# Moving one more group of transposed probabilities from ScalarE and VectorE to GpSimd in the dense attention heads of a two-layer diffusion step

## The chip, the cores and the metric

The kernel runs on one core of a Trainium2 chip. The metric is the time of one execution on the device in microseconds (us); the median of three runs of the kernel before is 3486.17 us.

Engines are named as in the profile: PE is TensorE's matrix products (PEld its weight loads), ACT is ScalarE, DVE is VectorE, POOL (or Pool) is GpSimd, SP issues most DMA transfers. Only ACT and DVE read PSUM in this kernel; Pool works on SBUF alone.

## The reference

Two layers run over 128 prompt tokens and 1024 sample tokens of width 1024. Each layer has an input projection, attention in 16 heads, an output projection and a gated FFN with a width-3 convolution. Six heads are neighbourhood attention (a window of keys for each query); the other ten, called dense here, attend to all keys:

```python
def blocked_attention(q, k, v):
    ...
    def one_block(q_blk):
        s = jnp.einsum('bqhgd,bkhd->bhgqk', q_blk, k).astype(jnp.float32) * scale
        p = jax.nn.softmax(s, axis=-1).astype(v.dtype)
        return jnp.einsum('bhgqk,bkhd->bqhgd', p, v)
```

For a sample token of a dense head there are 1152 keys: 128 cached context keys and 1024 sample keys. Four dense heads are latent attention ("MLA", with head width 96), six are grouped-query attention ("GQA", width 64). All is float32.

## The kernel before, in words

**Precision.** A product of float32 numbers is made of float32r parts: a number is split into a high part (a cast to float32r) and a low part (number minus high part). MLA scores take three products for each block of keys, GQA scores two. The probabilities are split too: both parts of their transpose, `PT[0]` and `PT[1]`, are multiplied with V.

**Phase B (attention, `phase_b`).** Heads follow each other: four MLA, six GQA, six neighbourhood. A dense head works on nine tiles of 128 queries: eight sample tiles in four pairs (tile a = 0 and a = 1 of a pair) and one prompt tile, which comes third. `step` (L915) emits the program for one tile after another in a software pipeline: scores of tile s, exponentials and normalisation of tile s-1, transposes of tile s-3, and pieces of the products with V of older pairs. The tile framework then sets the order of the instructions on each engine, so the order on an engine is not the order in the text of the program.

What a dense tile of 128 queries x 1152 keys needs:

- scores: PE writes 896 columns into a PSUM tile `SA` and 256 into `SB`; DVE takes the maxima (L712 over SA, L789 over SB, the second including the first);
- exponentials: ACT makes exp of SB and of SA into an SBUF tile `P` with sums (L699); Pool adds the two sums (`ssum`, L702); DVE takes the reciprocal (`rs`, L707); Pool multiplies P by it (L708, 1152 columns);
- transposes: PE transposes 128x128 blocks of P into a PSUM bank `T` (L719; two such banks, four blocks in each). The nine blocks of the two tiles of a pair make five groups: a = 0 has blocks 0 to 3 and 4 to 7, a = 1 has the same two, and the fifth group holds block 8 of both tiles (256 columns).
- evacuation of a group: four of the five go through `evac2` (L199): ACT casts T into the high part in PT (L202), DVE subtracts it from T into the low part (L203). The fifth goes `via` SBUF: ACT copies T into `rt` (L724), ACT casts rt into the high part (L194 in `split`), Pool subtracts into the low part (L197);
- products with V: for each block of keys one product for each part of PT, 256 queries wide (L737), into `O`; ACT copies one half of O (`otmp`, L742) and DVE adds the other (Y, L744).

A dense head thus has four via groups and sixteen `evac2` groups of 512 columns, and the prompt tile adds one group of 128 columns. In both layers there are 20 dense heads with 80 pairs.

Outside the dense heads the change touches nothing: neighbourhood heads call `transpose_p` without `via`, and `split` with `hi_eng=pool` has no other caller.

Of the kernel before, what the change touches and what calls it, by code (L numbers as in the profile page):

```python
# [14 lines left out]
F32 = mybir.dt.float32  # L15
# [10 lines left out]
D = 1024  # L26
# [19 lines left out]
def tile_kernel(ctx: ExitStack, tc: tile.TileContext, I, O):  # L46
# [13 lines left out]
    # ---- scratch in DRAM  # L60
    XD = [dram.tile([NTT, 128, D], F32, name=f"XD{i}") for i in range(2 * L - 1)]
    GD = [[dram.tile([2, KC, 128], F32, name=f"GD{l}{i}") for i in range(2)] for l in range(L)]
    # (the two parts of) queries and keys with features on rows, values with tokens on rows;
    # key columns: prompt, cached context, samples
# [7 lines left out]
    # ---- PSUM outside attention: six banks for products, two for transposes and small sums  # L72
# [30 lines left out]
    # ---- helpers  # L103
    nw = ctx.enter_context(tc.tile_pool(name="nw", bufs=3))

    def rsqrt_newton(v, n):
        """v: [128, n], f32; returns its rsqrt, times -8192."""
        u = nw.tile([128, 8], F32, name="nw_u")[:, :n]
        t = nw.tile([128, 8], F32, name="nw_t")[:, :n]
        dve.tensor_scalar(out=u.bitcast(I32), in0=v.bitcast(I32), scalar1=-0.5,  # L110
                          scalar2=float(0x5F3759DF), op0=ALU.mult, op1=ALU.add)
        # y -> y * (3 - y * y * v) / 2 on u = c * y
        c = 1.0
        for _ in range(3):
            if n == 1:
                dve.scalar_tensor_tensor(out=t, in0=u, scalar=u, in1=v, op0=ALU.mult, op1=ALU.mult)  # L116
            else:
                dve.tensor_tensor(out=t, in0=u, in1=u, op=ALU.mult)
                dve.tensor_tensor(out=t, in0=t, in1=v, op=ALU.mult)
            dve.scalar_tensor_tensor(out=u, in0=t, scalar=-3.0 * c * c, in1=u, op0=ALU.add, op1=ALU.mult)  # L120
            c *= -2.0 * c * c
        return u

    def squares(ss, i, src, junk):
        """Sums of squares over the features of a tile of tokens, in two halves, into ss[:, :, i]."""
        for j in range(2):
            act.activation(out=junk[j], in_=src[j], func=AF.Square, accum_out=ss[:, j, i:i + 1])

    def rsqrt_mean(ss, n):
        """From squares: rsqrt of the mean, times -256."""  # L130
        v = nw.tile([128, 8], F32, name="nw_v")[:, :n]
        dve.scalar_tensor_tensor(out=v, in0=ss[:, 0, :n], scalar=D * EPS, in1=ss[:, 1, :n],  # L132
                                 op0=ALU.add, op1=ALU.add)
        return rsqrt_newton(v, n)
# [4 lines left out]
    def h_group(p, tiles, xs, A, B, H, ht_w=256):  # L139
        """h = xs * A + B with features on partitions, in two float32r parts;  # L140
        xs[t]: the scaled tokens [128, D]."""
        hhi, hlo = H
        n, s = 128 * len(tiles), 1 if tiles[0] == 0 else 0
        cs = slice(tiles[0] * 128, tiles[0] * 128 + n)
        for m in range(KC):
            tp = aux()[:, :n]
            for i, t in enumerate(tiles):
                pe.transpose(tp[:, i * 128:(i + 1) * 128], xs[t][:, m * 128:(m + 1) * 128], ident)
            a, b = A[:, m, s:s + 1], B[:, m, s:s + 1]
            act.activation(out=hhi[:, m, cs], in_=tp, func=AF.Identity, scale=a, bias=b)  # L150
            ht = p.tile([128, ht_w], F32, name="ht", bufs=2)[:, :n]
            dve.tensor_scalar(out=ht, in0=tp, scalar1=a, scalar2=b, op0=ALU.mult, op1=ALU.add)
            (pool if m % 2 else dve).tensor_tensor(out=hlo[:, m, cs], in0=ht, in1=hhi[:, m, cs].bitcast(F32),  # L153
                                                   op=ALU.subtract)
            if m % 2:
                yield

    def norm_tiles(p, tiles, src, junk, w, xts, G, xout, A, B, H, xs, groups, eng):
        """x + norm(src) * G for tiles of tokens; lists by tile: src, junk (two halves each),
        w: scratch, then the scaled new x, xts: x; eng: the engines for the gates of each half. When a group of tiles is complete, h."""  # L160
# [38 lines left out]
    def evac2(hi, lo, src, scale=None):  # L199
        """The two parts of src * scale, src in PSUM."""  # L200
        if scale is None:
            act.copy(hi, src)  # L202
            dve.tensor_tensor(out=lo, in0=src, in1=hi.bitcast(F32), op=ALU.subtract)  # L203
        else:
            act.activation(out=hi, in_=src, func=AF.Copy, scale=scale)
            dve.scalar_tensor_tensor(out=lo, in0=src, scalar=scale, in1=hi.bitcast(F32),
                                     op0=ALU.mult, op1=ALU.subtract)

    # ---- adaLN modulation
# [22 lines left out]
    def late_consts(l, z):  # L232
        z.conv = lay.tile([128, 44, 4], F32, name="conv")
        nc.scalar.dma_start(out=z.conv, in_=I["conv"][l])
        z.gtok = lay.tile([128, 896], F32, name="gtok", bufs=1)
        nc.scalar.dma_start(out=z.gtok, in_=I["gtok"][l:l + 1, :].to_broadcast([128, 896]))
        # times -1 / 8192, and the scale of the scores
        for c0, c1, f in ((0, 384, 1.0), (384, 768, 0.125), (768, 896, 1.0)):
            pool.tensor_scalar(out=z.gtok[:, c0:c1], in0=z.gtok[:, c0:c1], scalar1=-f / 8192, scalar2=1.0,
                               op0=ALU.mult, op1=ALU.mult)  # L240

    def ada_done(z, part):
        """The gains and gates, times -1 / 256."""
        gi, dst = {1: (0, z.Am), 2: (1, z.Gm), 4: (2, z.Af), 5: (3, z.Gf)}.get(part, (None, None))
        if dst is not None:
# [5 lines left out]
            else:  # L251
                dve.scalar_tensor_tensor(out=dst, in0=z.mods[:, part], scalar=-1.0 / 256, in1=g,
                                         op0=ALU.mult, op1=ALU.mult)
                # as rows in DRAM
# [7 lines left out]
    def gate_rows(z, p, i):  # L262
        """[128, 2, D]: the gates of samples and prompt on every partition."""
        G = p.tile([128, 2, D], F32, name="G")
        load_gate_rows(z, G, i)
        return G
# [6 lines left out]
    def ada_bias(z, part, c, n, mp):  # L273
        """mods of n chunks of features from mp [128, n, 2] and the biases."""
# [3 lines left out]
    def ada_pe(l, z, p, part, q):  # L278
        """On the tensor engine, four chunks of features: where nothing else can run yet."""
# [14 lines left out]
    def ada_dve(l, z, p, parts, wd):  # L294
        """Sums over the chunks of features on the vector engine, over partitions on TensorE;
        wd columns at a time."""
# [24 lines left out]
    # ---- phase A: input projections  # L321
    def rope_rot(p, x, H, d, tabs, out, eng=dve):
        """x, out: [128, H, d] views; tabs: (cos, signed sin), [128, d] each."""
# [13 lines left out]
    def load_w(wp, src, tag, bufs, lo_eng=pool, wr=None):  # L337
        """The two parts of a block of weights, src [128, a, b]; wr: the pool of the raw ones."""
# [19 lines left out]
    def phase_a(l, z, H, w, before, rest):  # L358
        """w: the weights of the values; before(t): called before token tile t of H is first read;
        rest(): called when w is no longer used, returns the pool for the other weights."""  # L360
# [13 lines left out]
        # values of the grouped-query and the neighbourhood heads  # L374
# [22 lines left out]
        # multi-head latent attention  # L397
# [157 lines left out]
        # neighbourhood attention: q, k, features on partitions  # L555
        with tc.tile_pool(name="an", bufs=1) as p:
            # the cached context
# [57 lines left out]
    # ---- phase B: attention  # L615
    def phase_b(l, Y, kps, bp, pp, sp, bps):
# [5 lines left out]
        def alternating(name, shape):  # L622
            """In one of two pools, in turn."""
# [71 lines left out]
        def exps(P, mneg, pieces, sign):  # L695
            """exp(sign * src + mneg) into P; pieces: (src, first column). Returns the sums."""
# [17 lines left out]
        def transpose_p(blocks, outs, tag="T", via=False):  # L714
            """blocks: columns of P; outs: where they go, one after the other, in the two parts of PT;
            via: through SBUF, for Pool to take a share."""
# [5 lines left out]
            if via:  # L722
                rt = sp.tile([128, 256], F32, name="rt", bufs=2).rearrange("p (a b) -> p a b", b=128)
                act.copy(rt, src)  # L724
                split(rt, *outs)
            else:
                evac2(*outs, src)

        def pv_items(V, PT, slots, n, hg, t0):
            """slots: list of (V tile, PT slot)."""  # L730
# [22 lines left out]
        class Task:  # L753
            """One tile of queries: scores, maximum | exp, 1 / sum | transposes | products with V."""
# [19 lines left out]
            def dense(self, hd, pair, a):  # L774
# [19 lines left out]
                def tr(j):  # L794
                    if a == 0 and j == 0:
                        hd.PT[pair] = new_pt()
                    if j < 8:
                        transpose_p([self.block(j + i) for i in range(4)],
                                    [o[:, j:j + 4, qs] for o in hd.PT[pair]])
# [11 lines left out]
            def na(self, hd, pair, a):  # L811
# [23 lines left out]
                # the blocks of keys by slot of PT; within: the second tile of queries has no slot 4,  # L835
                # the first no slot 6
# [122 lines left out]
    # ---- phase C: output projection  # L959
# [5 lines left out]
    def phase_c(l, z, Y, yst, H, xin, xout, wp):  # L965
        """Returns the generators of the norms that are still to be finished, and their pool's stack."""
# [42 lines left out]
    # ---- phase D: gated ConvFFN  # L1009
    def phase_d(l, z, H, wp, pend, pend_done, last):  # L1010
        """pend: generators that finish the last tiles of H; pend_done(): called when they are,
        returns Y, the pools for convolutions and gated values and the generators to run along;
        last(t, down): called for each tile of Y, down(j) completes a half of it."""
# [15 lines left out]
        def shifted(acc, pts, m, c, sh):  # L1029
            """The products of chunk c, at the column after (sh = 1) or before (sh = -1) their own."""  # L1030
# [91 lines left out]
        # the last gated values chunk by chunk  # L1122
# [75 lines left out]
    def rest_of_norms(owner, gens, done):  # L1198
        """The remaining norms of the layer before, each tile's before it is read."""
# [182 lines left out]
```

## Time and profile before

| what | value |
|---|---|
| median of 3 runs | 3486.17 us (3481.18 to 3488.51) |
| span of the profiled execution | 3484.8 us, 50564 instructions |
| PE busy | 3299.9 us (95%) |
| PEld busy | 2964.7 us (85%) |
| DVE busy | 2220.3 us (64%) |
| ACT busy | 1485.6 us (43%) |
| POOL busy | 1087.5 us (31%) |
| mean granted clock of TensorE | 0.979 of full speed |

The profile is of one execution, whose span from first to last instruction is 3484.8 us, 1.4 us below the median of the runs; no other time of that execution is shown. The shares are over the whole span. The dense heads lie at about 364 to 660 us (layer 1) and 2081 to 2376 us (layer 2), some 17% of it; the rest is projections, neighbourhood heads and the FFN, where the engines stand in quite another proportion.

### The profile page before, as it was taken

The page shows a single profiled execution, that of the slowest core. Times are in us where ns is not written, and L with a number is a line of the kernel's source. Part 1 is how long each engine was busy: PE and PEld are TensorE (multiplying, and loading weights), DVE is VectorE, ACT ScalarE, POOL GpSimd, SP SyncE. Part 2 cuts the span into 40 slices and gives each one's busy share as a digit, 9 for nine tenths or more (in the row PEclk, how much of TensorE's full clock was granted, in tenths as well). Part 3 has the DMA queues.
Part 4 walks back from the last instruction along what each step waited for, and adds up shares of the span by engine and source line. Part 5 has one row for each costly group of instructions (what it writes and reads, how often), then busy time and mean ns, then how long its engine had stood idle before and what let it go on. Part 6 is the DMA issues. An engine that isn't in the chain of part 4 may idle for free. (4 is left out here: it accounts for less than half of the span.)

```text
span 3484.8 us, 50564 instructions
## 1 busy us (share of the span) xinstructions
PE 3299.9 (95%) x18540; PEld 2964.7 (85%) x18540; DVE 2220.3 (64%) x4915; ACT 1485.6 (43%) x3085; POOL 1087.5 (31%) x1063
## 2 busy tenths in 40 slices
PE   7989999999999999999989899999889999999996
PEld 3878888877899999999868789888779999999995
DVE  5785788887755555333588858888776533333437
ACT  4321788884422222222353228888743222222222
POOL 2121445541332223222231314554322222222223
PEclk9999999999999999999999999999999999999998
DMA  6467521453222122111245674215522111111113
GB/s 234 135 186 214 138 72 44 103 145 135 91 67 79 61 67 67 38 43 43 71 159 143 176 231 102 52 44 148 167 91 73 55 49 51 44 44 43 38 37 115
DMA packets 193416, 339.35 MB, mean 97 GB/s; under 512 B 18448, under 2 KB 107920, under 8 KB 193168
## 3 DMA queue, kind: packets, MB, share of 16 engines
q1 hardware_dynamic: 191872, 334.93, 32.6%
q8 instruction: 147, 2.41, 0.3%
q10 hardware_dynamic: 1296, 1.19, 0.1%
q14 instruction: 101, 0.83, 0.1%
HBM read 260.61 MB, written 75.43 MB: 96 GB/s over the span
## 5 line engine op out<-in xcount | busy, mean ns | idle before, releaser
L1025 PE MATMUL mm<-hhi,wu 128*128 128x384 f32 x4224 | 874.5, 336 | 7.3 <-DVE acc L1037 4.5
L1025 PEld LDWEIGHTS mm<-hhi,wu 128*128 128x128 f32 x4224 | 746.4, 188 | 14.5 <-DVE acc L1037 5.0
L1037 DVE SCALAR_TENSOR_TENSOR acc<-mm,conv,acc 128x127 f32<-128x127 f32 (+2 forms) x704 | 314.1, 509 | 359.3 <-ACT acc L1042 359.2
L1072 PE MATMUL aux<-wd,g 128*128 128x512 f32 x2160 | 498.0, 390 | 0.0
L1025 PE MATMUL mm<-hlo,wu 128*128 128x384 f32 x2112 | 496.8, 335 | 0.0
L1072 PEld LDWEIGHTS aux<-wd,g 128*128 128x128 f32 x2160 | 404.7, 188 | 83.1 <-DVE g L1061 0.4
L1025 PEld LDWEIGHTS mm<-hlo,wu 128*128 128x128 f32 x2112 | 379.0, 188 | 0.7 <-DVE hlo L153 0.4
L197 POOL TENSOR_TENSOR wu<-wraw,wu 128x1024 fp32r<-128x1024 f32 x90 | 220.8, 2455 | 442.6 <-ACT wu L194 439.9
L737 PE MATMUL O<-PT,V 128*128 128x256 f32 (+1 forms) x2080 | 345.6, 294 | 6.9 <-DVE Y L744 4.5
L1077 DVE TENSOR_TENSOR Y<-Y,aux 128x512 f32<-128x512 f32 x324 | 220.8, 686 | 200.8 <-PE aux L1072 200.7
L708 POOL TENSOR_SCALAR P<-P,rs 128x1152 f32<-128x1152 f32 (+3 forms) x288 | 290.6, 1010 | 149.8 <-DVE rs L707 123.8
L719 PE MATMUL T<-ident,P 128*128 128x128 f32 x1856 | 299.1, 277 | 17.1 <-DVE PT L203 12.3
L689 PE MATMUL SA<-k,q 128*128 128x512 f32 (+5 forms) x1224 | 301.0, 366 | 8.1 <-ACT ko L611 3.9
L203 DVE TENSOR_TENSOR PT<-T,PT 128x512 fp32r<-128x512 f32 (+1 forms) x448 | 290.3, 656 | 24.9 <-ACT PT L202 18.8
L197 POOL TENSOR_TENSOR wd<-wraw,wd 128x1024 fp32r<-128x1024 f32 x46 | 111.2, 2417 | 612.8 <-ACT wd L194 612.8
L737 PEld LDWEIGHTS O<-PT,V 128*128 128x128 f32 x2080 | 276.7, 189 | 22.3 <-DVE Y L744 10.3
L194 ACT CAST wd<-wraw 128x1024 fp32r<-128x1024 f32 x50 | 52.4, 1050 | 527.9 <-PE aux L1072 400.5
L202 ACT CAST PT<-T 128x512 fp32r<-128x512 f32 (+1 forms) x448 | 247.7, 568 | 55.7 <-PE T L719 42.5
L308 DVE SCALAR_TENSOR_TENSOR aacc<-wadv,sc,aacc 128x512 f32<-128x512 f32 x280 | 234.5, 870 | 46.8 <-DMA wadv<-w_ada 46.7
L719 PEld LDWEIGHTS T<-ident,P 128*128 128x128 f32 x1856 | 213.3, 141 | 58.1 <-DVE PT L203 16.0
L689 PEld LDWEIGHTS SA<-k,q 128*128 128x128 f32 (+1 forms) x1224 | 198.7, 192 | 33.5 <-ACT P L699 6.8
L712 DVE TENSOR_REDUCE mx<-SA 128x1 f32<-128x896 f32 (+1 forms) x192 | 182.3, 950 | 34.5 <-PE SA L689 34.5
(222 smaller groups left out, 5181.9 us busy)
## 6 DMA issues: line engine op xcount, KB each, us to landing
wraw<-w_up SPq DMA_DIRECT2D x88, 512.0 KB, 3.5
wadv<-w_ada SPq DMA_DIRECT2D x160, 256.0 KB, 3.0
wraw<-w_down SPq DMA_DIRECT2D x44, 512.0 KB, 3.5
k<-KT SPq DMA_DIRECT2D x64, 320.0 KB, 5.6
q<-QT SPq DMA_DIRECT2D x48, 288.0 KB, 6.0
XD<-xt SPq DMA_DIRECT2D x27, 512.0 KB, 3.2
xt<-XD SPq DMA_DIRECT2D x27, 512.0 KB, 4.0
wraw<-w_in SPq DMA_DIRECT2D x24, 512.0 KB, 4.0
```

Source lines behind the costliest of these rows:

```text
L197: (lo_eng or pool).tensor_tensor(out=lo, in0=raw, in1=hi.bitcast(F32), op=ALU.subtract)
L202: act.copy(hi, src)
L203: dve.tensor_tensor(out=lo, in0=src, in1=hi.bitcast(F32), op=ALU.subtract)
L308: dve.scalar_tensor_tensor(out=accs[i], in0=w, scalar=sc[:, k, i:i + 1], in1=accs[i], op0=ALU.mult, op1=ALU.add)
L689: pe.matmul(out, q[0:rows, qc:qc + 128], kview(k[0:rows]), start=(i == 0), stop=(i == len(passes) - 1))
L708: pool.tensor_scalar(out=P[:, :n], in0=P[:, :n], scalar1=rs, scalar2=1.0, op0=ALU.mult, op1=ALU.mult)
L719: pe.transpose(tp[:, j * 128:(j + 1) * 128], p, ident)
L737: pe.matmul(op[0][:, :n], V[:, vt, :], PT[e][:, sl, :n], start=(i == 0 and e == 0), stop=(i == last and e == 1))
L1025: pe.matmul(pts[c][:, :CN], a[:, k, :], h_[:, k, c * CN:(c + 1) * CN], start=(k == 0 and a is whi and h_ is hhi), stop=(k == KC - 1 and a ...
L1037: dve.scalar_tensor_tensor(out=d, in0=pts[c][:, lo_ - c * CN:hi_ - c * CN], scalar=cw[:, wi:wi + 1], in1=d, op0=ALU.mult, op1=ALU.add)
L1072: pe.matmul(pt, g[:, ts], d[:, 0, js], start=(n == 0), stop=(n == tot - 1))
L1077: dve.tensor_tensor(out=Y[:, t, js], in0=Y[:, t, js], in1=pt, op=ALU.add)
```

## The change

In the dense heads a second group of each pair goes through SBUF: blocks 4 to 7 of tile a = 0 (512 columns). For via groups, old and new, the high part is now made by Pool (`hi_eng=pool`, a `tensor_copy`, L196) rather than by ACT. `rt` grows from 256 to 512 columns, still with two buffers. Comments and docstrings are removed elsewhere, which moves line numbers by one at most.

```diff
             if via:
-                rt = sp.tile([128, 256], F32, name="rt", bufs=2).rearrange("p (a b) -> p a b", b=128)
+                rt = sp.tile([128, 512], F32, name="rt", bufs=2).rearrange("p (a b) -> p a b", b=128)
+                rt = rt[:, :len(blocks)]
                 act.copy(rt, src)
-                split(rt, *outs)
+                split(rt, *outs, hi_eng=pool)
             else:
                 evac2(*outs, src)
...
                     if j < 8:
                         transpose_p([self.block(j + i) for i in range(4)],
-                                    [o[:, j:j + 4, qs] for o in hd.PT[pair]])
+                                    [o[:, j:j + 4, qs] for o in hd.PT[pair]], via=a == 0 and j == 4)
```

`split` itself is unchanged:

```python
    def split(raw, hi, lo, hi_eng=None, lo_eng=None):
        if hi_eng is None:
            act.copy(hi, raw)
        else:
            hi_eng.tensor_copy(hi, raw)
        (lo_eng or pool).tensor_tensor(out=lo, in0=raw, in1=hi.bitcast(F32), op=ALU.subtract)
```

The order on Pool, in a GQA head of the first layer, from one normalisation to a sum of a later tile. Before (L197 of 256 columns is the fifth group of a pair):

```order
L708 TENSOR_SCALAR P<-P,rs 128x1152
L197 TENSOR_TENSOR PT_5562<-rt,PT_5561 128x256
L702 TENSOR_TENSOR ssum<-ssum 128x1
L708 TENSOR_SCALAR P<-P,rs 128x1152
L702 TENSOR_TENSOR ssum<-ssum 128x1
L708 TENSOR_SCALAR P<-P,rs 128x1152
L197 TENSOR_TENSOR PT_5659<-rt,PT_5658 128x256
```

and with the change, for the same pair (its PT tiles are numbered 5597 and 5598 here) and the next:

```order
L196 CAST PT_5597<-rt 128x4x128
L197 TENSOR_TENSOR PT_5598<-rt,PT_5597 128x4x128
L702 TENSOR_TENSOR ssum<-ssum 128x1
L708 TENSOR_SCALAR P<-P,rs 128x1152
L196 CAST PT_5597<-rt 128x256
L197 TENSOR_TENSOR PT_5598<-rt,PT_5597 128x256
L702 TENSOR_TENSOR ssum<-ssum 128x1
L708 TENSOR_SCALAR P<-P,rs 128x1152
L196 CAST PT_5696<-rt 128x4x128
L197 TENSOR_TENSOR PT_5697<-rt,PT_5696 128x4x128
L702 TENSOR_TENSOR ssum<-ssum 128x1
```

Both instructions of the new group stand behind one tile's normalisation and ahead of the next sum; the cast and the subtraction of the fifth group stand between the other normalisation and the other sum.

The order on DVE for the same pair, before:

```order
L707 RECIPROCAL rs<-ssum 128x1
L203 TENSOR_TENSOR PT_5562<-T,PT_5561 128x4x128 x2
L712 TENSOR_REDUCE mx<-SA 128x1
L707 RECIPROCAL rs<-ssum 128x1
L203 TENSOR_TENSOR PT_5562<-T,PT_5561 128x4x128
L744 TENSOR_TENSOR Y<-O,otmp 64x256
L789 ISA junk,mx<-SB,zeros,mx 128x256
L789 ISA mx 128x1
L203 TENSOR_TENSOR PT_5562<-T,PT_5561 128x4x128
L712 TENSOR_REDUCE mx<-SA 128x1
```

and with the change:

```order
L203 TENSOR_TENSOR PT_5598<-T,PT_5597 128x4x128
L712 TENSOR_REDUCE mx<-SA 128x1
L707 RECIPROCAL rs<-ssum 128x1
L203 TENSOR_TENSOR PT_5598<-T,PT_5597 128x4x128
L745 TENSOR_TENSOR Y<-O,otmp 64x256
L790 ISA junk,mx<-SB,zeros,mx 128x256
L790 ISA mx 128x1
L203 TENSOR_TENSOR PT_5598<-T,PT_5597 128x4x128
L712 TENSOR_REDUCE mx<-SA 128x1
L707 RECIPROCAL rs<-ssum 128x1
L790 ISA junk,mx<-SB,zeros,mx 128x256
```

One subtraction (L203) of four is gone; the reciprocals still stand ahead of the other subtractions and of the maximum over SB (L789, now L790) that the next exponentials wait for.

## Rows read from the trace of the kernel before

**Rows 1.** Stretches: us; busy PE, PEld, DVE, ACT, POOL (count); clock, DMA, GB/s: MLA, GQA.

```profile
428.30:459.20 30.90, 30.40 (x224) 27.91 (x223) 25.29 (x57) 25.36 (x65) 14.71 (x22) 1.00 0.34 84
...
548.50:577.00 28.50, 27.49 (x198) 24.35 (x197) 25.00 (x56) 25.30 (x65) 14.68 (x21) 1.00 0.31 69
```

**Rows 2.** Waits in four GQA heads (519.6 to 634.6 us): us, times, longest.

```profile
POOL ssum L702 <- ACT P L699: 28.6, 30, 2.7
...
DVE rs L707 <- POOL ssum L702: 5.8, 14, 0.7
```

**Rows 3.** Pool's instructions in the GQA head of 548.5 us, in order of time (start, duration).

```profile
551.45 0.19 POOL L702 TENSOR_TENSOR ssum<-ssum 128x1 f32<-128x1 f32 x1 [2.56 <-ACT P L699]
...
554.39 0.19 POOL L702 TENSOR_TENSOR ssum<-ssum 128x1 f32<-128x1 f32 x1 [1.15 <-ACT P L699]
...
557.39 0.19 POOL L702 TENSOR_TENSOR ssum<-ssum 128x1 f32<-128x1 f32 x1 [0.19 <-ACT P L699]
...
560.45 0.19 POOL L702 TENSOR_TENSOR ssum<-ssum 128x1 f32<-128x1 f32 x1 [0.86 <-ACT P L699]
...
564.73 0.19 POOL L702 TENSOR_TENSOR ssum<-ssum 128x1 f32<-128x1 f32 x1 [0.26 <-ACT P L699]
...
567.16 0.19 POOL L702 TENSOR_TENSOR ssum<-ssum 128x1 f32<-128x1 f32 x1 [0.70 <-ACT P L699]
567.65 1.24 POOL L708 TENSOR_SCALAR P<-P,rs 128x1152 f32<-128x1152 f32 x1 [0.30 <-DVE rs L707]
569.76 0.73 POOL L197 TENSOR_TENSOR PT<-rt,PT 128x256 fp32r<-128x256 f32 x1 [0.88 <-ACT PT L194]
571.21 0.19 POOL L702 TENSOR_TENSOR ssum<-ssum 128x1 f32<-128x1 f32 x1 [0.72 <-ACT P L699]
571.78 1.23 POOL L708 TENSOR_SCALAR P<-P,rs 128x1152 f32<-128x1152 f32 x1 [0.37 <-DVE rs L707]
573.64 0.19 POOL L702 TENSOR_TENSOR ssum<-ssum 128x1 f32<-128x1 f32 x1 [0.63 <-ACT P L699]
```

**Rows 4.** DVE in the same head, in order of time.

```profile
567.38 0.16 DVE L707 RECIPROCAL rs<-ssum 128x1 f32<-128x1 f32 x1
...
568.52 0.47 DVE L789 CUSTOM_DVE_ANT_0 junk<-SB,zeros,mx 128x256 f32<-128x256 f32 x1
...
573.86 0.16 DVE L707 RECIPROCAL rs<-ssum 128x1 f32<-128x1 f32 x1 [0.73 <-POOL ssum L702]
```

**Rows 5.** ACT in the same head, in order of time.

```profile
568.87 0.37 ACT L724 COPY rt<-T 128x256 f32<-128x256 f32 x1 [0.31 <-PE T L719]
569.27 0.41 ACT L194 CAST PT<-rt 128x256 fp32r<-128x256 f32 x1
569.59 0.47 ACT L699 ACTIVATE P<-SB,mx 128x256 f32<-128x256 f32 x1
```

**Rows 6.** Groups by form, DVE, four GQA heads (519.6 to 634.6 us): busy, mean ns | idle before.

```profile
L203 DVE TENSOR_TENSOR PT<-T,PT 128x512 fp32r<-128x512 f32 x64 | 43.2, 686 | 3.1 <-ACT PT L202 2.2
```

**Rows 7.** Groups by form, Pool, whole span.

```profile
L708 POOL TENSOR_SCALAR P<-P,rs 128x1152 f32<-128x1152 f32 x160 | 196.8, 1230 | 74.5 <-DVE rs L707 62.9 <-PE T L719 6.6 <-PE SA L689 4.9
...
L197 POOL TENSOR_TENSOR PT<-rt,PT 128x256 fp32r<-128x256 f32 x80 | 58.7, 734 | 71.5 <-ACT PT L194 67.4 <-DVE PT L203 4.0
...
L708 POOL TENSOR_SCALAR P<-P,rs 128x768 f32<-128x768 f32 x48 | 43.6, 909 | 28.6 <-DVE rs L707 25.3 <-PE O L737 2.8 <-DMA bedge<-b_full 0.5
...
L708 POOL TENSOR_SCALAR P<-P,rs 128x128 f32<-128x128 f32 x32 | 11.9, 372 | 16.3 <-PE O L737 9.3 <-DVE rs L707 6.2
...
L197 POOL TENSOR_TENSOR ck<-ck,ck 128x512 fp32r<-128x512 f32 x2 | 2.6, 1284 | 19.0 <-DMA cr<-c_krT 19.0
...
L619 POOL MEMSET zeros<- 128x256 f32 x2 | 0.6, 312 | 79.3 <-PE mm L586 79.3
```

**Rows 8.** Waits of PE and its weight loads in three MLA heads (397 to 490 us).

```profile
PEld T L719 <- DVE PT L203: 2.9, 5, 0.7
...
PE T L719 <- DVE PT L203: 1.4, 6, 0.3
```

## The prediction

> **What bounds the kernel now.** I read the busy time by stretch first, since the change acts in the dense heads alone and the shares over the whole span say nothing of them. A GQA head takes 28.5 us and an MLA head 30.9 us [rows 1]; the granted clock is 1.00 in both, the level of 2.4 GHz, so no part of the argument hangs on TensorE's clock. Six GQA and four MLA heads in two layers make 12 and 8. In a GQA head DVE is busy for 25.0 us, ACT for 25.3 and PE for 27.5 (its ends are modelled, and its weight loads take 24.4): three engines at 85 to 97%, none full, Pool at 14.7 of 28.5 (52%). So what bounds such a head is a loop between the engines, each of which takes its work in a fixed order.
>
> The waits [rows 2] and the instructions in order of time [rows 3 to 5] show the loop. Pool waits for ACT's exponentials before it can add the sums (28.6 us in four heads), DVE waits at its reciprocal for Pool's sum (5.8 us, 14 times), and what stands behind the reciprocal on DVE waits too: the subtractions that free T, and the maximum over SB that the next exponentials need. One turn for a tile is: maximum (DVE), exponentials (ACT), sum (Pool), reciprocal (DVE), subtraction, next maximum. The starts of Pool's sums [rows 3] show its length: 551.45, 554.39, 557.39, 560.45, 564.73, 567.16, 571.21, 573.64, so intervals of 2.94, 3.00, 3.06, 4.28, 2.43, 4.05 and 2.43 us, and the eighth, over the prompt tile to the next head, is what is left of 28.5 to 28.9, about 6.5. A pair takes 4.05 + 2.43 = 6.48 us in the steady part. Pool is idle for most of it, yet it stands in the loop: a sum that comes late delays DVE at once.
>
> **The change, part by part.** There are 80 pairs, four in each of 20 dense heads.
>
> *Removed from DVE:* a subtraction of 512 columns in each pair, 0.69 us [rows 6], 80 x 0.69 = 55 us in all, 2.7 us of a head's 25.0. *Removed from ACT:* the second copy of the fifth group, 0.41 us [rows 5], 33 us in all. The copy of the new group out of PSUM takes the place of a cast of the same size: nothing. It frees the bank T without DVE, which helps PE's next transposes. PE and the DMA queues issue the same instructions as before; rt's further 256 columns cost nothing that a row shows.
>
> *Added to Pool:* in each pair a cast of 512 columns, one of 256, and a subtraction of 512. The subtraction has a row of its own kind, 1.28 us [rows 7]. Pool casts nothing in the kernel before, so the casts are bounded. The nearest rows are Pool's other operations with one input, the multiplications: 372, 909 and 1230 ns for 128, 768 and 1152 columns, so 0.84 ns per column; on that line 512 columns take 0.69 us and 256 take 0.48. That is what I take. Below lies a memset, which reads nothing: 0.31 us for 256 columns, and with the same slope 0.53 for 512. Above lies the subtraction with two inputs, 1.28 and 0.73 us. Added: 0.69 + 0.48 + 1.28 = 2.45 us in a pair, 196 us in all, 9.8 us in a head; Pool goes from 14.7 to 24.5 of 28.5 us.
>
> For this price the Trainium skill has a rule, on its page GPSIMD Engine Reference, section "Elementwise — side-by-side cycle accounting": VectorE at its plain rate and Pool both process 128 float32 values per cycle, which at the 1.2 GHz of the page's Specifications makes 0.43 us for 512 columns without any fixed part. By that estimate the sum below would be about +16 instead of +29 us; no run so far shows such a cast.
>
> *Where it lies.* By the order on Pool, the cast and subtraction of the new group (0.69 + 1.28 = 1.97 us) stand between one tile's normalisation and the next tile's sum. So in that interval Pool has to do, after a sum: the trip over the reciprocal to the normalisation (571.21 to 571.78, 0.57 us [rows 3]), the normalisation (1.23), then 1.97: 3.77 us before the next sum can start. The interval was 2.43: **1.34 us longer**. DVE stands at the reciprocal meanwhile (its wait there was 0.73 us [rows 4] and grows), and behind it are the subtraction, the maximum over SB, and ACT's next exponentials.
>
> In the other interval of the pair Pool does 0.49 + 1.24 + 0.48 + 0.73 = 2.94 us, less than the 4.05 there are; that one is set by DVE and ACT, and there the relief counts: the exponentials started at 569.59 behind two copies of ACT, though the maximum was done at 569.0 (568.52 + 0.47 [rows 4, 5]). With one copy they can start at about 569.14: **0.45 us shorter**. DVE's removed subtraction stood ahead of the reciprocal that now waits for Pool anyway, so it is worth nothing there. A steady pair: +1.34 - 0.45 = +0.89 us.
>
> *The sum.* A GQA head has two such pairs (4.28 + 2.43 and 4.05 + 2.43): +1.8. The interval of 3.06 after the prompt tile also gets a new group: 3.77 - 3.06 = +0.7. The fourth new group falls in the long interval of some 6.5 us, where Pool's work (0.49 + 1.23 + 0.37 for the prompt + 1.21 + 1.97 = 5.3 us) fits; there the relief of DVE and ACT can show, between 0 and the 0.69 of DVE's subtraction: I take -0.4, a little over the middle. So +2.1 us a head, 12 x 2.1 = +25 us.
>
> In an MLA head PE has more to do (27.9 us of weight loads against 24.4 [rows 1]) while DVE and ACT have the same, so the same loop has 2.4 us more room. The gain there is at most PE's wait for the banks that DVE frees, 2.9 + 1.4 us in three heads, 1.4 us a head [rows 8]; the loss at most the 2.1 of a GQA head. I take +0.5, near the middle of -0.7 (half of that wait) and +2.1: 8 x 0.5 = +4 us.
>
> Sum: +29 us on the span of 3484.8, 3513.8. The median of the runs is 1.4 us above that span, so 3515 us on their scale.
>
> **The rivals.**
>
> *Relief wins (faster).* The Trainium skill's Perfetto Trace Analysis page, section "Optimizing Scalar/DVE Operations", says that where DVE is saturated, handing some of its work even to GpSimd may make sense. As a mechanism of this kernel: ACT and DVE lose 1.6 and 2.7 us of a GQA head, the bank T is free without DVE, and Pool does its 24.5 us in what were idle times. A floor for Pool is four pairs of 2 x (0.49 + 1.23) + 3.18 = 6.62 us and 0.37 for the prompt, 26.9 us, so a GQA head could shorten by 1.6 at most; half of it is -0.8 x 12 = -10 us, and a third of PE's 1.4 us in MLA heads is -0.5 x 8 = -4: 3472 us. For it: PE waits for DVE's subtractions in every stage of the heads. Against it: Pool would have to run almost without a gap, in an order in which its sums wait for ACT and its normalisations for DVE. It decides if the 512-column cast and subtraction start as soon as rt is written, that is if the normalisation ahead of them is over by then.
>
> *Given and taken (no change).* If the late sum finds DVE busy with what it would do anyway, the intervals change by +0.4 and -0.4; 3486 us, within 7 us. The long interval over the prompt tile is where this could happen for more than one pair.
>
> *A cast on Pool costs what a subtraction does (slower still).* Then 0.59 us more lie in each lengthened interval, three in each of 20 heads, 60 x 0.59 = +35: 3550 us.
>
> *The change doesn't do what it says:* excluded, since the order shows 160 casts and 80 more subtractions on Pool, and 80 subtractions fewer on DVE.
>
> **How the numbers follow.** The forecast (Pool's sums late, casts near 0.69 and 0.48 us): 0.60. Casts at the price of a subtraction: 0.07. No change: 0.15. Relief wins: 0.18. About 0.2% (7 us) is what a measurement can tell from no change. So faster 0.18, same 0.15, slower 0.67. The range reaches down to 3470, which takes in the rival without change and about half of the faster one, and up to 3550, the end with dear casts; within it the forecast's own is 3493 to 3536 (MLA heads at -0.7 or +2.1 each move it by -10 or +13, casts as cheap as a memset by 60 x 0.16 = -10, no relief over the prompt tile by +5).
>
> **What would show it.** Right: GQA heads of 30 to 31 us; Pool's busy time up by some 196 us with casts near 0.69 and 0.48; DVE's wait at the reciprocal for Pool well above 5.8 us in four heads, ACT's exponentials waiting longer for DVE's maximum, and pairs in which one sum follows the other by about 3.8 us. Wrong: GQA heads of 28 us or less with Pool over 85% busy, Pool's sums still waiting for ACT, and DVE's wait at the reciprocal unchanged. If MLA heads grow as much as GQA heads, my share for them was too small.

## The result, and the profile after

| | before | after |
|---|---|---|
| median of 5 runs each | 3486.17 us (3475.65 to 3492.05) | 3510.95 us (3508.73 to 3516.7) |
| span of the profiled execution | 3484.8 us | 3511.5 us |

The changed kernel is slower: the ratio is 1.0069 [1.0056, 1.0083], 24.8 us between the medians. The forecast was 3515.

The head of the page after, with span and busy times:

```profile
span 3511.5 us, 50694 instructions
...
PE 3300.5 (94%) x18540; PEld 2965.0 (84%) x18540; DVE 2171.1 (62%) x4835; ACT 1465.1 (42%) x3005; POOL 1264.4 (36%) x1303
```

DVE lost 49 us of work, ACT 21, Pool got 177 more, PE has the same. The work that was moved is off the two engines, and the span grew by 26.7 us.

The stretches of one MLA and one GQA head after (us; busy time of PE, PEld, DVE, ACT, POOL with counts; clock, DMA share, GB/s):

```profile
433.30:465.30 32.00, 30.58 (x225) 28.05 (x224) 23.03 (x54) 24.56 (x61) 23.62 (x34) 1.00 0.33 81
...
553.70:584.10 30.40, 27.50 (x200) 24.30 (x199) 22.91 (x53) 24.39 (x61) 23.64 (x34) 1.00 0.28 63
```

Beside [rows 1], DVE is down by some 2.2 us a head and Pool up by 9; the clock is still 1.00 and PE's busy time is the same, yet the GQA head takes 30.4 us instead of 28.5 and the MLA head 32.0 instead of 30.9. No engine does more than 28 of those 30.4 us: the head waits.

For what, the waits in four GQA heads after (523.6 to 644.6 us; us, times, longest) show:

```profile
DVE rs L707 <- POOL ssum L702: 17.9, 24, 2.2
ACT rt L725 <- PE T L719: 11.7, 21, 1.0
PEld T L719 <- DVE PT L203: 11.2, 12, 1.3
...
POOL ssum L702 <- ACT P L699: 7.4, 16, 0.9
...
PE T L719 <- DVE PT L203: 6.9, 8, 1.0
```

The two waits of [rows 2] have changed places. Pool waited 28.6 us for the exponentials and now waits 7.4; DVE waited 5.8 us for Pool's sum and now waits 17.9. And PE's transposes and their weight loads, whose bank of the new group is now free without DVE, wait 6.9 and 11.2 us (2.5 and 2.5 before) for DVE's other subtractions: these stand behind the reciprocal that waits for the sum. ACT in turn waits 11.7 us (4.4 before) for the transposes that it copies to `rt`.

Pool in the head of 553.7 us, in order of time (start, duration, and in brackets the idle time before):

```profile
560.88 0.61 POOL L196 CAST PT<-rt 128x512 fp32r<-128x512 f32 x1 [1.20 <-ACT rt L725]
561.58 1.28 POOL L197 TENSOR_TENSOR PT<-rt,PT 128x512 fp32r<-128x512 f32 x1
562.82 0.20 POOL L702 TENSOR_TENSOR ssum<-ssum 128x1 f32<-128x1 f32 x1
...
574.88 0.20 POOL L702 TENSOR_TENSOR ssum<-ssum 128x1 f32<-128x1 f32 x1 [0.39 <-ACT P L699]
575.13 0.40 POOL L196 CAST PT<-rt 128x256 fp32r<-128x256 f32 x1
575.61 0.73 POOL L197 TENSOR_TENSOR PT<-rt,PT 128x256 fp32r<-128x256 f32 x1
576.32 1.24 POOL L708 TENSOR_SCALAR P<-P,rs 128x1152 f32<-128x1152 f32 x1
577.50 0.62 POOL L196 CAST PT<-rt 128x512 fp32r<-128x512 f32 x1
578.20 1.28 POOL L197 TENSOR_TENSOR PT<-rt,PT 128x512 fp32r<-128x512 f32 x1
579.44 0.19 POOL L702 TENSOR_TENSOR ssum<-ssum 128x1 f32<-128x1 f32 x1
...
582.93 0.19 POOL L702 TENSOR_TENSOR ssum<-ssum 128x1 f32<-128x1 f32 x1 [0.25 <-ACT P L699]
583.50 1.23 POOL L708 TENSOR_SCALAR P<-P,rs 128x1152 f32<-128x1152 f32 x1 [0.37 <-DVE rs L707]
584.67 0.61 POOL L196 CAST PT<-rt 128x512 fp32r<-128x512 f32 x1
585.37 1.28 POOL L197 TENSOR_TENSOR PT<-rt,PT 128x512 fp32r<-128x512 f32 x1
586.62 0.19 POOL L702 TENSOR_TENSOR ssum<-ssum 128x1 f32<-128x1 f32 x1
```

Where a sum has no bracket, Pool ran into it without a gap from the cast and subtraction of 512 columns: at 562.82, 579.44 and 586.62. Before the last two ACT's exponentials had been done for 1.2 and 0.9 us. At 560.88 Pool had first waited 1.20 us for ACT's copy, with the sum queued behind. DVE on the other side of the last two:

```profile
579.67 0.16 DVE L707 RECIPROCAL rs<-ssum 128x1 f32<-128x1 f32 x1 [0.96 <-POOL ssum L702]
579.75 0.67 DVE L203 TENSOR_TENSOR PT<-T,PT 128x512 fp32r<-128x512 f32 x1
...
586.84 0.16 DVE L707 RECIPROCAL rs<-ssum 128x1 f32<-128x1 f32 x1 [2.11 <-POOL ssum L702]
586.92 0.67 DVE L203 TENSOR_TENSOR PT<-T,PT 128x512 fp32r<-128x512 f32 x1
```

DVE stands still for 0.96 and 2.11 us, each time with a subtraction behind it that would free a bank T.

The heads, from one prompt tile's scores to the next: the five full GQA steps of each layer took 28.66 us on average before and 30.27 after. The table below gives the eight intervals between the starts of Pool's sums in such a head, as means over ten heads; the long one, over the prompt tile, is first. A star marks intervals at whose end Pool has the cast and subtraction of 512 columns ahead of the sum (in the changed kernel).

| kernel | long* | 2 | 3 | 4* | 5 | 6* | 7 | 8* | sum |
|---|---|---|---|---|---|---|---|---|---|
| before | 6.44 | 2.94 | 2.95 | 3.13 | 4.30 | 2.43 | 4.06 | 2.42 | 28.7 |
| after | 6.46 | 3.57 | 2.65 | 3.68 | 2.10 | 4.56 | 3.54 | 3.68 | 30.2 |
| `sums_first` (below) | 6.23 | 3.72 | 2.64 | 3.11 | 3.27 | 2.99 | 3.69 | 2.79 | 28.4 |
| `relief_only` (below) | 6.34 | 3.71 | 2.76 | 2.84 | 2.84 | 3.34 | 3.68 | 2.70 | 28.2 |

Intervals 4, 6 and 8 became longer by 0.55, 2.13 and 1.26 us, some of which the intervals beside them gave back.

### The profile page after: what moved, and what is told of

Read it like the earlier page. It is cut to its first block, busy times and chain, and to the rows that moved or that the text cites. A ratio compares the mean times of both kernels' runs of the same rounds, so it can differ in the third digit from the quotient of the medians.

```text
span 3511.5 us, 50694 instructions
## 1 busy us (share of the span) xinstructions
PE 3300.5 (94%) x18540; PEld 2965.0 (84%) x18540; DVE 2171.1 (62%) x4835; ACT 1465.1 (42%) x3005; POOL 1264.4 (36%) x1303
## 5 line engine op out<-in xcount | busy, mean ns | idle before, releaser
L1026 PEld LDWEIGHTS mm<-hhi,wu 128*128 128x128 f32 x4224 | 745.3, 188 | 11.7 <-DVE acc L1038 4.8
L197 POOL TENSOR_TENSOR wu<-wraw,wu 128x1024 fp32r<-128x1024 f32 x90 | 220.5, 2452 | 441.9 <-ACT wu L194 439.1
L197 POOL TENSOR_TENSOR wd<-wraw,wd 128x1024 fp32r<-128x1024 f32 x46 | 111.2, 2418 | 609.2 <-ACT wd L194 609.2
L689 PE MATMUL SA<-k,q 128*128 128x512 f32 (+5 forms) x1224 | 309.6, 370 | 6.0 <-ACT ko L611 3.9
L203 DVE TENSOR_TENSOR PT<-T,PT 128x512 fp32r<-128x512 f32 (+1 forms) x368 | 235.6, 647 | 17.6 <-ACT PT L202 14.6
L202 ACT CAST PT<-T 128x512 fp32r<-128x512 f32 (+1 forms) x368 | 203.3, 560 | 64.1 <-PE T L719 54.2
```

The source lines that it names most:

```text
L197: (lo_eng or pool).tensor_tensor(out=lo, in0=raw, in1=hi.bitcast(F32), op=ALU.subtract)
L689: pe.matmul(out, q[0:rows, qc:qc + 128], kview(k[0:rows]), start=(i == 0), stop=(i == len(passes) - 1))
L1026: pe.matmul(pts[c][:, :CN], a[:, k, :], h_[:, k, c * CN:(c + 1) * CN], start=(k == 0 and a is whi and h_ is hhi), stop=(k == KC - 1 and a ...
```

## The experiments

Three theories stood against each other. **A, the late sum**: the time is lost because Pool's new work stands ahead of the sums in Pool's fixed order. **B, the load on Pool**: 177 us more on Pool cost time wherever they stand. **C, the order on the other engines**: with the new planning PE, ACT and DVE do their work in a less fortunate order. The kernel before is timed beside each group of runs; its median was 3486.47 us for the first four and 3488.01 for the last four, which ran on another chip. Each time is followed by its ratio to that median, with its interval; runs of different groups are best compared by these ratios.

### The sums on DVE (`after_sum_dve`) and the same in the kernel before (`before_sum_dve`)

```diff
-                pool.tensor_tensor(out=ssum[:, 0:1], in0=ssum[:, 0:1], in1=ssum[:, 1:2], op=ALU.add)
+                dve.tensor_tensor(out=ssum[:, 0:1], in0=ssum[:, 0:1], in1=ssum[:, 1:2], op=ALU.add)
```

> The changed kernel, with the two partial sums added on DVE rather than on Pool; all of Pool's new work stays. Theory A (late sum: the new cast and subtraction stand ahead of a sum on Pool for which DVE's reciprocal waits): DVE no longer waits for Pool, its wait at the reciprocal for Pool goes from 18.3 us in four GQA heads to none, heads fall to 28.5 us or less, the time to 3465 to 3490 us. Theory B (load: Pool has too much to do, wherever the sum is added): Pool still has some 22 us of work in a head and its normalisations come late, GQA heads stay near 30 us, 3500 to 3515 us.

Measured: 3494.81 us, 1.0020 [1.0009, 1.0032], between the two ranges. GQA heads take 29.0 us, MLA heads 31.4.

> The kernel before, with the sums added on DVE; the control for the run with the change. Theory A: Pool's turn in the loop (0.19 us and two handovers for each tile) goes, DVE gets a short instruction more: 0 to -20 us against 3486. Theory B: Pool was half idle, so nothing changes: 3480 to 3492 us.

Measured: 3489.71 us, 1.0011 [1.0002, 1.0021]: the gain that A had for this kernel did not come. In the changed kernel the edit gives back 16 us, in the kernel before it costs 3: sums that don't stand in Pool's queue are worth 19 us only where Pool's new work stands there. That speaks for A, but not all of the loss came back, and the edit also changes DVE's order, so C was not out. The waits of this kernel in four GQA heads (518.6 to 634.8 us) show what else is in Pool's queue:

```profile
POOL P L708 <- DVE rs L707: 13.6, 17, 1.1
POOL PT L196 <- ACT rt L725: 13.1, 16, 2.2
...
PEld T L719 <- DVE PT L203: 6.6, 12, 0.9
```

Pool now waits 13.1 us at the casts for ACT's copies, with normalisations queued behind them. The wait of DVE for a sum of Pool's is gone, since there is none, and PE's wait for DVE's subtractions fell from 11.2 to 6.6 us.

### The new group without Pool's casts (`hi_on_act`)

```diff
-                split(rt, *outs, hi_eng=pool)
+                split(rt, *outs)
```

> The new group alone: a second group of each pair goes through SBUF, with the high parts made by ACT as before, so that Pool adds only the 512-column subtraction. Theory A: still 1.28 us ahead of the sum, the interval is at least 0.57 + 1.23 + 1.28 = 3.1 us where it was 2.43, and ACT has a cast of about 0.6 us more in each pair: 3495 to 3515 us. Theory B: Pool has 14.7 + 5.1 = 19.8 us in a head of 28.5 and is far from full: 3475 to 3490 us.

Measured: 3497.67 us, 1.0032 [1.0021, 1.0043]; GQA heads 29.7 us, MLA heads 31.7. The stretch of one GQA head, and two waits of four (519.9 to 638.8 us):

```profile
549.80:579.40 29.60, 27.66 (x200) 24.39 (x199) 22.92 (x53) 27.77 (x69) 19.50 (x26) 1.00 0.24 52
```

```profile
POOL PT L197 <- ACT PT L194: 14.3, 24, 1.5
...
DVE rs L707 <- POOL ssum L702: 12.4, 12, 2.0
```

Pool's block is shorter, but it waits for ACT's cast (14.3 us) with the sums behind it, and ACT is now busy for 27.8 of 29.6 us. Half of the loss stays, in A's range and not in B's, but part of it may be ACT's, and the framework's order on PE and DVE is another one too: this run alone would not have told these apart.

### Pool's casts without the new group (`fifth_only`)

```diff
-                                    [o[:, j:j + 4, qs] for o in hd.PT[pair]], via=a == 0 and j == 4)
+                                    [o[:, j:j + 4, qs] for o in hd.PT[pair]])
```

> The other half alone: the high part of the fifth group on Pool (256 columns), no new group. Theory A: 0.40 us more on Pool in the interval that has room (4.05 us, Pool's work 2.9), ACT's 0.41 us saved ahead of the exponentials: 3470 to 3486 us. Theory B: Pool at 16.3 us of 28.5, about no change: 3480 to 3490 us. A rival to both, that any other order which the framework picks costs some 20 us, would show here as 3500 us or more.

Measured: 3480.12 us, 0.9980 [0.9968, 0.9993], a little faster than before; GQA heads 28.15 us, MLA heads 31.1. So this half of the change is a gain of some 6 us, and the new group costs some 31. With only a cast of 256 columns more on Pool, DVE waits 3.7 us for the sums in four heads (5.8 before).

### The same work on Pool, behind the sum (`sums_first`)

The cast and subtraction of both kinds of via groups are held back, and put into Pool's queue behind the sum of the next step. The instructions of the changed kernel are all there, and the order on PE, DVE and ACT is the same as in it, instruction by instruction; only Pool's order differs.

```diff
-                pool.tensor_tensor(out=ssum[:, 0:1], in0=ssum[:, 0:1], in1=ssum[:, 1:2], op=ALU.add)
+                count["sum"] = pool.tensor_tensor(out=ssum[:, 0:1], in0=ssum[:, 0:1], in1=ssum[:, 1:2],
+                                                  op=ALU.add)
...
-                split(rt, *outs, hi_eng=pool)
+                late.append(lambda: split(rt, *outs, hi_eng=pool))
...
+        def flush():
+            with tc.issue_after(count["sum"].ins):
+                while late:
+                    late.pop(0)()
...
             if prev:
                 prev.exp()
+            if late:
+                flush()
+            if prev:
                 prev.norm()
```

> The changed kernel with the same instructions; a group's cast and subtraction on Pool are queued behind the next tile's sum instead of ahead of it. On PE, ACT and DVE every instruction stands where it stood; Pool's order alone differs. Theory A (late sum): DVE's wait at the reciprocal falls from 18 us in four GQA heads to 7 or less, GQA heads go from 30.2 us to 29.0 or less, as with the sum on DVE; 3475 to 3497 us. Theory B (load: Pool's 23.5 us of a head are too many in any order): 3503 to 3515 us. Theory C (the order that the framework now gives to PE, ACT and DVE is the worse one): nothing changes, since that order stays: 3505 to 3515 us.

Measured: 3478.53 us (3474.76 to 3487.25), 0.9979 [0.9966, 0.9993]. GQA heads take 28.4 us, MLA heads 31.1. The stretch of a GQA head, Pool in it in order of time, and the waits of four GQA heads (518.9 to 632.6 us; the edit moves line numbers by one to three):

```profile
547.30:575.70 28.40, 27.34 (x199) 24.31 (x198) 22.89 (x53) 24.25 (x61) 23.11 (x34) 1.00 0.26 59
```

```profile
570.97 0.19 POOL L702 TENSOR_TENSOR ssum<-ssum 128x1 f32<-128x1 f32 x1 [0.41 <-ACT P L699]
571.10 0.61 POOL L196 CAST PT<-rt 128x512 fp32r<-128x512 f32 x1
571.78 1.29 POOL L197 TENSOR_TENSOR PT<-rt,PT 128x512 fp32r<-128x512 f32 x1
573.05 1.23 POOL L709 TENSOR_SCALAR P<-P,rs 128x1152 f32<-128x1152 f32 x1
574.60 0.19 POOL L702 TENSOR_TENSOR ssum<-ssum 128x1 f32<-128x1 f32 x1 [0.32 <-ACT P L699]
```

```profile
POOL ssum L702 <- ACT P L699: 15.5, 28, 1.5
DVE rs L708 <- POOL ssum L702: 8.7, 14, 1.3
...
PEld T L722 <- DVE PT L203: 2.2, 9, 0.4
```

Pool does as much as in the changed kernel (23.1 us of a head against 23.6), and the same instructions stand in the same order everywhere else; the loss of 25 us is gone, and some 7 more. The sums wait for the exponentials again, as before, DVE's wait for them has halved, and PE's wait at its transposes' weight loads for DVE fell from 11.2 to 2.2 us. B and C can't explain this, A does. In the table's terms, behind the sum means in the next interval: in each pair the group of 512 columns now lies in the interval that had room (5 and 7, 4.30 and 4.06 us before) and the group of 256 in the tight one (6 and 8, 2.43 us before). The price is that the normalisation now starts late, behind the subtraction: at 573.05, though DVE's reciprocal for it began at 571.30 and took 0.15 us. But that delay is cheap here: the largest wait of a kind that was not there before is one of 3.0 us in the same four heads, of the products with V for Pool's low parts.

### Only the new group behind the sum (`sums_first_512`)

As above, but the groups of 256 columns stay where the change has them:

```diff
-                late.append(lambda: split(rt, *outs, hi_eng=pool))
+                if len(blocks) == 4:
+                    late.append(lambda: split(rt, *outs, hi_eng=pool))
+                else:
+                    split(rt, *outs, hi_eng=pool)
```

> The same for the new group alone; the fifth group's cast and subtraction stay where the changed kernel has them, in the interval that had room. Theory A: nearly all of the gain of sums_first, within 6 us of it, since the fifth group's 1.1 us were not late; B and C: 3503 to 3515 us.

Measured: 3493.57 us, 1.0020 [1.0007, 1.0032], and GQA heads of 29.4 us: a miss. Pool in order of time shows why:

```profile
569.71 0.20 POOL L702 TENSOR_TENSOR ssum<-ssum 128x1 f32<-128x1 f32 x1 [0.43 <-ACT P L699]
569.84 0.61 POOL L196 CAST PT<-rt 128x512 fp32r<-128x512 f32 x1
570.53 1.29 POOL L197 TENSOR_TENSOR PT<-rt,PT 128x512 fp32r<-128x512 f32 x1
571.81 1.23 POOL L709 TENSOR_SCALAR P<-P,rs 128x1152 f32<-128x1152 f32 x1
572.98 0.40 POOL L196 CAST PT<-rt 128x256 fp32r<-128x256 f32 x1
573.47 0.73 POOL L197 TENSOR_TENSOR PT<-rt,PT 128x256 fp32r<-128x256 f32 x1
574.16 0.19 POOL L702 TENSOR_TENSOR ssum<-ssum 128x1 f32<-128x1 f32 x1
```

The new group follows its sum, but pushes the normalisation back, and the other group, still ahead of the next sum, is pushed back with it: both groups lie between the same two sums, 4.45 us without a gap. In the ten heads of the table this is interval 7, and interval 2 holds both groups too: they take 4.44 and 4.33 us, against 3.69 and 3.72 in `sums_first`, where each of them holds one group. What counts is not one block's place but how much Pool has to do between one sum and the next. This is the theory of the late sum again, with the wrong culprit named in what I expected.

### The relief without Pool's work (`relief_only`)

For the new group ACT casts T into the high part, and Pool fills the low part with zeros (0.53 us instead of a cast and a subtraction). The low part of 80 of the 320 groups of 512 columns is left out of the computation. The fifth group is as in the change.

```diff
-            if via:
+            if via and len(blocks) == 4:
+                act.copy(outs[0], src)
+                pool.memset(outs[1].bitcast(F32), 0.0)
+            elif via:
```

> The changed kernel without the new group's low part: ACT casts T straight into the high part, Pool clears the low part with a memset (left out: the low part of 80 of the 320 groups of 512 columns), the fifth group as in the change. DVE and the bank T are relieved as in the change, and Pool pays some 0.5 us in place of 1.9, without waiting for ACT. It shows what the relief is worth. Theory A and B: with Pool's price gone the relief shows, 0.5 to 1.5 us a head on top of the fifth group's gain: 3455 to 3475 us. Theory C: 3485 us or more, as the order on PE, ACT and DVE is again the framework's for a group less on DVE.

Measured: 3479.16 us, 0.9974 [0.9964, 0.9984]: a miss, since I had expected a gain for DVE's 55 us. The stretch of one GQA head and waits of four (515.9 to 628.8 us):

```profile
544.10:572.40 28.30, 27.09 (x200) 24.30 (x199) 23.21 (x53) 24.22 (x62) 18.36 (x30) 1.00 0.26 60
```

```profile
DVE rs L707 <- POOL ssum L702: 7.4, 12, 1.2
DVE mx L712 <- PE SA L689: 6.4, 8, 0.8
POOL PT L724 <- PE O L741: 5.7, 12, 0.6
```

The heads (28.21 us) are as long as those of `fifth_only` (28.15 us), where DVE does all of these subtractions: taking them away from DVE is worth nothing that these runs can tell. The order on PE and DVE is that of the changed kernel, and on ACT too, with a cast in the place of each copy; so theory C, which had 3485 us or more, fails here as well. In `fifth_only` DVE waits 2.2 us for PE's scores in four heads, here 6.4. PE is busy for 27.1 of 28.3 us: what DVE gains it spends waiting for PE and for the sums (7.4 us, against 3.7 in `fifth_only`). The price on Pool is not quite gone, which I had overlooked: the zeros wait 5.7 us for the products with V that still read the low part, with Pool's sums queued behind them. A version without even the zeros on Pool was not tried, so the relief alone has no clean price.

### Only the fifth group, behind the sum (`fifth_sums_first`)

The edits of `fifth_only` and of `sums_first` together.

> The fifth group's high part on Pool and no new group, with its cast and subtraction queued behind the next sum. Theory A: DVE's wait at the reciprocal was only 3.7 us in four GQA heads with the fifth group alone, so little is left to gain: 3472 to 3483 us. Theory B and C: as without the queueing, 3475 to 3485 us.

Measured: 3481.92 us, 0.9982 [0.9972, 0.9991]; GQA heads 28.3 us, DVE's wait for the sums 3.7 us in four heads, as in `fifth_only`. With a block of 256 columns alone Pool has time enough between two sums, and its place costs and gives nothing that these runs can tell. Beside `sums_first` this is a second comparison with and without the new group, now with Pool's work behind the sums in both: heads of 28.4 and 28.3 us, so there too DVE's 55 us less bring no gain.

## Why the prediction came out

**What bounds the heads: right.** The prediction called it a loop between the engines in which Pool's sum stands though Pool is half idle. `sums_first` shows it: Pool's order alone decides over some 31 us (1.0069 against 0.9979 of the time before). The prediction went too far in one word: in the steady pair Pool is not idle "for most of it" but for some 45%. And one of its signs did not come: ACT's exponentials hardly wait longer for DVE's maximum (3.3 us in four GQA heads before, 3.7 after). The late reciprocal reaches ACT through the bank T, by DVE's subtraction and PE's transposes, which the prediction had named as the first of the two things behind the reciprocal.

**The price of the casts: right on the path, for a reason I did not have.** The groups of Pool after:

```profile
L197 POOL TENSOR_TENSOR PT<-rt,PT 128x512 fp32r<-128x512 f32 x80 | 102.7, 1283 | 6.7
...
L196 POOL CAST PT<-rt 128x512 fp32r<-128x512 f32 x80 | 49.1, 613 | 30.9 <-ACT rt L725 30.5
```

A cast of 512 columns takes 0.61 us and one of 256 took 0.40, where I took 0.69 and 0.48 from the line of the multiplications [rows 7]. But Pool stands idle for 0.08 us between its cast and the subtraction that reads it (6.7 us over 80), so on the path they came to 0.70 and 0.48, and Pool's busy time grew by 177 us instead of 196. The rival in which a cast costs what a subtraction does (1.28) falls. From 256 to 512 columns the cast grows by 0.84 ns per column, with 0.18 us beside that. The Trainium skill's GPSIMD Engine Reference page (section "Performance versus the Vector engine", just above the one that the prediction names) gives, as an estimate from its figures, 0.43 us for the 512 columns alone, 0.83 ns each. The trace agrees on that slope with its 0.84; the sum by that page, as in the prediction, left out the fixed part and the wait.

Two sums of the prediction are off by a little, and nothing rests on them. By its own count of 60 lengthened intervals, casts of 0.43 us make the sum smaller by 16 us, that is +13 and not +16. And the terms that it lists for its own forecast span some 3495 to 3533 us, not 3493 to 3536.

**The steady pair: right as worked out, but only one of two is steady.** I gave the tight interval 3.77 us and the roomy one 4.05 - 0.45 = 3.60; intervals 8 and 7 of the table measure 3.68 and 3.54, so that pair grew by 0.74 (0.89 predicted), and its last part runs 583.50, 584.67, 585.37, 586.62, as added up. The other pair did not grow: 4.30 + 2.43 became 2.10 + 4.56. There the exponentials of the first tile came early enough for its sum at 574.88, and Pool then did both groups in one stretch. This is the rival "given and taken", in one pair of two.

**The interval after the prompt: right** (3.13 to 3.68, +0.55, predicted +0.7). **The long interval: wrong.** I took -0.4 for the relief there; it went from 6.44 to 6.46. I had added up Pool's work in it (5.3 us) but not Pool's wait there for ACT's copy, 1.20 us at 560.88 and 1.23 on average in the ten heads; together they fill the interval, and the sum at its end starts without a gap. And intervals 2 and 3, which I had left alone, grew by 0.33 together. So a GQA head grew by 1.6 us, not 2.1, and the last of each layer, which runs over into a neighbourhood head, by 0.6 and 0.4 up to its last sum: **the mis-sized term is GQA's**, 10 x 1.61 + 1.0 = +17 us instead of +25.

**MLA heads: too small.** They took +0.9 us each, +7.4 for the eight (predicted +0.5 and +4). I had set the growth against a gain of half of PE's wait for DVE's banks [rows 8]. Those waits of 2.9 and 1.4 us did not fall, they rose. The waits of three MLA heads after (397.8 to 493.2 us):

```profile
DVE rs L707 <- POOL ssum L702: 6.4, 8, 1.7
PEld T L719 <- DVE PT L203: 4.8, 6, 1.2
PE T L719 <- DVE PT L203: 4.4, 7, 0.8
```

The subtractions that free a bank stand behind the late reciprocal there too.

The sum: 17 + 7.4 = +24.5 us in the dense heads, beside +24.8 between the medians and the +29 forecast. Taken whole, from the first sum to the last, the dense heads of the two layers grew by 12.6 and 12.9 us. The two terms erred in opposite directions, and so did the parts of a GQA head (a pair that did not grow, against a relief that did not come): that the total lies so close is in part luck.

**The rival "relief wins"** needed Pool's block to start as soon as `rt` is written and to hold up nothing. In the framework's order it does hold up the sums. In `sums_first` it does so far less (8.7 us of DVE's waiting in four heads instead of 17.9), and heads become 0.2 to 0.3 us shorter than before, where that rival had 0.8. Even then the relief of DVE is not what wins: `fifth_only`, without it, has heads of 28.15 us, and `relief_only`, without Pool's subtraction, of 28.21. So the advice of the Perfetto Trace Analysis page of the Trainium skill ("Optimizing Scalar/DVE Operations"), that handing work to GpSimd may make sense where DVE is saturated, finds no support here: DVE was 88% busy in a head, and 55 us less work for it brought no gain that these runs can tell. The same section warns that Pool and DVE share a read port to SBUF. The trace shows nothing of that for this operation, which takes only one of its two inputs from SBUF: DVE's subtractions took 686 ns before [rows 6], and with Pool 1.6 times as busy beside them, in the group of four GQA heads after (523.6 to 644.6 us), 680:

```profile
L203 DVE TENSOR_TENSOR PT<-T,PT 128x512 fp32r<-128x512 f32 x49 | 33.0, 680 | 1.3 <-ACT PT L202 1.2
```

**A version that beats both** is `sums_first`: all of the change's work, 0.9979 [0.9966, 0.9993] of the time before and some 31 us less than the change. `fifth_only`, which leaves the new group with ACT and DVE, is level with it and smaller.

## What to carry to other kernels

An engine that is half idle is not free: ask which small instruction of its queue others wait for, and how much it has to do between one such instruction and the next. Sums of 0.2 us behind blocks of 2 us cost this kernel 25 us. The same blocks queued behind the sums, where the next interval has room for them, cost nothing, as long as only the long interval held two of them (`sums_first` against `sums_first_512`). And ask of the work that you take off an engine whether the loop waits for it: here DVE was 88% busy, and 55 us off it brought nothing that the runs could tell.

## What was not expected of the hardware

In the changed kernel Pool stands idle for 0.08 us between each cast and the subtraction that reads what the cast wrote (577.50 + 0.62 to 578.20; 0.079 to 0.086 us in all 160 pairs). Where an instruction does not read what the one before wrote, it mostly starts 0.02 to 0.06 us before the recorded end of that one (576.32 + 1.24 to 577.50).
